# A 4096 x 4096 x 4096 matrix product with leaky ReLU: first rows of A transposed in fp32 in place of bf16 and laid out in plain rows, and one late store issued whole

## The chip, the cores and the metric

The kernel runs on one core of a Trainium2 chip. The metric is the device time of one execution in microseconds (us), lower is better. A run's profile gives in addition the span of one execution, about 1.8 us shorter than the time of that execution. Engines are named as in the profile: PE does matrix products, with its weight loads shown apart as PEld, DVE, ACT and POOL work on vectors, SP issues transfers. PE writes its results into the memory PSUM; SBUF is the memory from which it reads. The pitch of equal instructions is the time from the start of one to the start of the next.

## The reference

```python
def setup_inputs():
    m, k, n = 4096, 4096, 4096
    return {"a": randn(m, k) as float32, "b": randn(k, n) as float32, "alpha": float32(0.01)}

def reference(a, b, alpha):
    x = np.matmul(a, b)
    return np.where(x > 0, x, alpha * x)
```

The product may be computed in bf16. PE multiplies by a stationary operand that has to hold A transposed, so A is rounded to bf16 and turned on the chip.

## The kernel before

The output is made in regions of 512 x 1024; PE does 8192 matmuls of 128 x 128 by 128 x 512. Nearly all of A comes in by transfers that round on the way, and is turned by DVE. Only the first 512 x 1024 of A, with the first 1024 rows of B, take another way, because nothing can start without them: they come in as fp32 by four and eight transfers of 512 KB on the SP queue (the last of B in two halves), alternating until A is done. Each of the four row tiles of A is rounded on DVE, turned by eight PE transposes into PSUM, and copied to SBUF, half by ACT and half by DVE.

```python
ident = small_pool.tile([P, P], BF16, name="ident")
...
a_rounded = at_pool.tile([P, MT, kw0], BF16, name="a_rounded", tag="at")
order = [("a", 0), ("b", 0), ("a", 1), ("b", 1), ("a", 2), ("b", 2), ("a", 3)]
...
turned = {(i, half): psum_pool.tile([P, kc0 // 2, P], BF16, name="turned", tag="ps") ...}

def round_a(i):
    nc.vector.tensor_copy(a_rounded[:, i, :], a_in[:, i, :])

def turn_a(i):
    cols = a_rounded[:, i, :].rearrange("m (p c) -> m c p", c=kc0)
    for c in range(kc0):
        nc.tensor.transpose(turned[i, 2 * c // kc0][:, c % (kc0 // 2), :], cols[:, c, :], ident)
    for half, copy in ((0, nc.scalar.copy), (1, nc.vector.tensor_copy)):
        to = a0[:, half * kc0 // 4:(half + 1) * kc0 // 4, i * P:(i + 1) * P, :]
        copy(to.rearrange("p c m e -> p c e m"),
             turned[i, half].rearrange("p (c e) m -> p c e m", e=2))
...
# the end of each region, for each of its four row tiles
for nt in range(NP):
    cols = slice(nt * NT, (nt + 1) * NT)
    nc.scalar.activation(o[:, cols], banks[mt, nt], LRELU, alpha=alpha)
    if final:
        nc.sync.dma_start(to[:, cols], o[:, cols])
if not final:
    nc.scalar.dma_start(to, o)
```

The tile `a0` keeps two chunks of the contraction interleaved, element by element (its last axis, `e`, is 2). So the copy writes every second 2-byte element. `final` marks the last region of all, whose stores go out in halves on SP.

## Time and profile before

| what | before |
|---|---|
| time, median of 3 runs | 1785.22 us (1784.99 to 1785.26) |
| span of the profiled run | 1783.7 us |
| PE busy | 99% of the span |

The prediction shows the lines of the page and of the timeline. Read them with one question: what has to be over before PE can run without a gap, and what comes after its last matmul? The change can act only there. The chain of work that ended last (start, duration, what), in the stretch that the change touches:

```profile
1.65 6.05 DMA a_in<-in_a_dram
...
7.73 0.70 DVE a_rounded L261
...
8.48 0.72 PE turned L266 x8
...
9.22 0.73 DVE at L269
9.95 0.30 DVE bt L276
...
10.26 0.70 DVE a_rounded L261
...
14.04 0.42 PE turned L266 x4
...
14.48 0.74 ACT at L269
...
15.27 8.61 PE ps L148 x39
```

The chain starts at the landing of the second tile of A, and it goes through DVE three times: cast, copy, cast. The other is the list of waits on the SP queue near the end (who waited for whom: total us, times, longest):

```profile
SPq L424 <- DMA out_dram<-o: 1.6, 1, 1.6
```

After its last store SP waits 1.6 us for stores to land.

### The profile page before, as it was taken

The page shows a single profiled execution, that of the slowest core. Times are in us where ns is not written, and L with a number is a line of the kernel's source. Part 1 is how long each engine was busy: PE and PEld are TensorE (multiplying, and loading weights), DVE is VectorE, ACT ScalarE, POOL GpSimd, SP SyncE. Part 2 cuts the span into 40 slices and gives each one's busy share as a digit, 9 for nine tenths or more (in the row PEclk, how much of TensorE's full clock was granted, in tenths as well). Part 3 has the DMA queues.
Part 4 walks back from the last instruction along what each step waited for, and adds up shares of the span by engine and source line. Part 5 has one row for each costly group of instructions (what it writes and reads, how often), then busy time and mean ns, then how long its engine had stood idle before and what let it go on. Part 6 is the DMA issues. An engine that isn't in the chain of part 4 may idle for free.

```text
span 1783.7 us, 17979 instructions
## 1 busy us (share of the span) xinstructions
PE 1766.8 (99%) x8070; PEld 804.6 (45%) x8234; DVE 156.3 (9%) x121; ACT 152.2 (9%) x270; POOL 360.3 (20%) x663
## 2 busy tenths in 40 slices
PE   9999999999999999999999999999999999999999
PEld 4444444444444444444444444444444444444444
DVE  5530000032000000002200000000220000000000
ACT  2010000000000000000000000000000000000001
POOL 4630210433002020143201202014320110301000
PEclk9999999999999999999999999999999999999999
DMA  9994653988039164397704917449860581835511
GB/s 260 191 253 111 116 133 86 190 127 126 39 94 189 48 120 117 94 198 127 124 24 96 187 48 143 93 105 201 131 119 12 114 170 48 168 68 123 113 48 47
DMA packets 147164, 214.06 MB, mean 120 GB/s; under 512 B 12816, under 2 KB 76304, under 8 KB 147088
## 3 DMA queue, kind: packets, MB, share of 16 engines
q0 software_dynamic: 126208, 139.50, 48.3%
q10 hardware_dynamic: 17856, 65.02, 9.3%
q1 hardware_dynamic: 3024, 8.39, 1.2%
q8 instruction: 64, 1.05, 0.2%
q14 instruction: 12, 0.10, 0.0%
HBM read 285.21 MB, written 67.11 MB: 198 GB/s over the span
## 4 chain that ended last, share of the span: by engine, by line
PE 99%; issue 1%; DMA 0%; DVE 0%; ACT 0%; SPq 0%
PE ps L148 99%; DMA a_in<-in_a_dram 0%; PE turned L266 0%; ACT at L269 0%; DVE a_rounded L261 0%; DVE at L269 0%; ACT o L388 0%; SPq L248 0%; SPq L246 0%; DVE bt L276 0%
## 5 line engine op out<-in xcount | busy, mean ns | idle before, releaser
L148 PE MATMUL ps<-bt,at 128*128 128x512 bf16 x8028 | 1760.4, 379 | 10.1 <-ACT bt L276 0.6
L148 PEld LDWEIGHTS <-at 128*128 128x128 bf16 x8192 | 801.2, 98 | 968.2 <-ACT at L269 2.6
L138 POOL DMA_DIRECT2D bt<-in_b_dram x408 | 217.1, 538 | 1084.4 <-PE ps L148 895.6
L388 ACT ACTIVATE o<-ps 128x512 f32<-128x512 f32 x240 | 130.7, 595 | 1524.4 <-PE ps L148 1450.4
L121 DVE STREAM_TRANSPOSE at<-a 128x1024 uint32<-128x1024 uint32 (+1 forms) x63 | 123.0, 1989 | 1136.2 <-PE ps L148 1113.8
L116 POOL DMA_DIRECT2D a<-in_a_dram x248 | 142.4, 581 | 203.1 <-DVE at L121 139.0
L225 DVE TENSOR_TENSOR part<-ps,part 128x512 f32<-128x512 f32 x32 | 20.3, 682 | 32.0 <-PE ps L148 32.0
L228 ACT ACTIVATE o<-part 128x1024 f32<-128x1024 f32 x8 | 8.5, 1058 | 77.2 <-DVE part L225 64.6
L223 ACT COPY part<-ps 128x512 f32<-128x512 f32 x8 | 4.4, 593 | 15.1 <-PE ps L148 12.4
L221 DVE COPY part<-ps 128x512 f32<-128x512 f32 x8 | 5.1, 671 | 4.8 <-PE ps L148 4.8
L276 ACT CAST bt<-b_in 128x512 bf16<-128x512 f32 x8 | 4.8, 617 | 2.0 <-DMA b_in<-in_b_dram 2.0
L84 PE MATMUL ps<-w 128*128 128x512 bf16 x8 | 3.6, 631 | 1.2 <-DVE x L80 1.2
L266 PE MATMUL turned<-ident,a_rounded 128*128 128x128 bf16 x32 | 2.8, 230 | 1.6 <-DVE a_rounded L261 1.5
L266 PEld LDWEIGHTS <-a_rounded 128*128 128x128 bf16 x32 | 2.4, 148 | 3.6 <-DVE a_rounded L261 3.4
L276 DVE CAST bt<-b_in 128x512 bf16<-128x512 f32 x8 | 3.4, 430 | 3.7 <-DMA b_in<-in_b_dram 3.7
L269 ACT COPY at<-turned 128x512 bf16<-128x512 bf16 x4 | 2.9, 729 | 8.6 <-PE turned L266 8.6
L269 DVE COPY at<-turned 128x512 bf16<-128x512 bf16 x4 | 2.9, 734 | 3.6 <-PE turned L266 3.6
L261 DVE CAST a_rounded<-a_in 128x1024 bf16<-128x1024 f32 x4 | 2.8, 698 | 4.1 <-DMA a_in<-in_a_dram 4.0
L315 POOL CAST x<-bt 128x1 f32<-128x1 bf16 x1 | 0.2, 183 | 11.5 <-ACT bt L276 11.5
L84 PEld LDWEIGHTS <-w 128*128 128x128 bf16 x8 | 1.0, 142 | 2.8 <-issue 1.6
L81 ACT ACT_TABLE_LOAD x1 | 1.3, 1283 | 0.7 <-PEq L410 0.7
L301 PE MATMUL ps<-w 128*128 128x512 bf16 x2 | 0.6, 379 | 0.0
(10 smaller groups left out, 1.6 us busy)
## 6 DMA issues: line engine op xcount, KB each, us to landing
bt<-in_b_dram POOLq DMA_DIRECT2D x408, 256.0 KB, 7.8
out_dram<-o ACTq DMA_DIRECT2D x124, 512.0 KB, 2.9
a<-in_a_dram POOLq DMA_DIRECT2D x248, 128.0 KB, 5.2
b_in<-in_b_dram SPq DMA_DIRECT2D x7, 512.0 KB, 9.8
a_in<-in_a_dram SPq DMA_DIRECT2D x4, 512.0 KB, 6.8
out_dram<-o SPq DMA_DIRECT2D x8, 256.0 KB, 2.0
b_in<-in_b_dram SPq DMA_DIRECT2D x2, 256.0 KB, 10.5
```

The lines of the kernel that those rows point to most:

```text
L84: nc.tensor.matmul(wp, w[:, :P], w, start=True, stop=True)
L116: nc.gpsimd.dma_start(to, src.rearrange("(g i) w -> i g w", i=32))
L121: nc.vector.transpose(dst.rearrange("p c m e -> p c (m e)").bitcast(U32) .rearrange("p c (g i) -> p g c i", i=32), held[0][:, 4 * t0:4 * t ...
L138: nc.gpsimd.dma_start(new_b(pi, u)[:, c0 + c, :], b_rows(n, s, c))
L148: nc.tensor.matmul(ps, at[mb, h, u][:, c // 2, mt * P:(mt + 1) * P, c % 2], bt[pi, u][:, c, nt * NT:(nt + 1) * NT], start=first, stop=last,)
L221: nc.vector.tensor_copy(kept, banks[mt, nt])
L225: nc.vector.tensor_add(kept, banks[mt, nt], kept)
L228: nc.scalar.activation(o, part[h][:, mt, :], LRELU, alpha=alpha)
L266: nc.tensor.transpose(turned[i, 2 * c // kc0][:, c % (kc0 // 2), :], cols[:, c, :], ident)
L269: copy(to.rearrange("p c m e -> p c e m"), turned[i, half].rearrange("p (c e) m -> p c e m", e=2),)
L276: copy(b0[:, i, columns(nt)], b_in[i][:, columns(nt)])
L388: nc.scalar.activation(o[:, cols], banks[mt, nt], LRELU, alpha=alpha)
```

## The change

The intent: spare the cast of A on DVE by turning the fp32 values as they lie, and round them where they have to be copied anyway, out of PSUM. The turned tile gets its chunks side by side, so the copies write plain rows. Apart from that, the first row tile of the last region is stored whole on the ACT queue.

```diff
-    ident = small_pool.tile([P, P], BF16, name="ident")
+    ident = small_pool.tile([P, P], FP32, name="ident")
@@ matmul: the first tile is read as plain rows
+            plain(t)[:, c, rows] if (mb, h, u) == (0, 0, 0) else t[:, c // 2, rows, c % 2],
@@ PSUM tiles of the transposes
-        (i, half): psum_pool.tile([P, kc0 // 2, P], BF16, name="turned", tag="ps")
+        (i, half): psum_pool.tile([P, kc0 // 2, P], FP32, name="turned", tag="ps")
@@ no cast
-    def round_a(i):
-        nc.vector.tensor_copy(a_rounded[:, i, :], a_in[:, i, :])
     def turn_a(i):
-        cols = a_rounded[:, i, :].rearrange("m (p c) -> m c p", c=kc0)
+        cols = a_in[:, i, :].rearrange("m (p c) -> m c p", c=kc0)
 ...
-            copy(to.rearrange("p c m e -> p c e m"), turned[i, half].rearrange(...))
+            copy(plain(a0)[:, c:c + kc0 // 2, i * P:(i + 1) * P], turned[i, half])
@@ stores
-                        if final:
+                        if final and mt:
                             nc.sync.dma_start(to[:, cols], o[:, cols])
-                    if not final:
+                    if not final or mt == 0:
                         nc.scalar.dma_start(to, o)
```

(Shortened: `plain` is the view of the tile with its chunks side by side.)

More of the change, by code (lines that the diff above doesn't have):

```diff
@@ L145, in pieces_b, with plain @@
         return [lambda c=c: load_b(pi, pairs[pi], s, c) for c in range(SEGS[s][2])]
+    def plain(t):
+        return t.rearrange("p c m e -> p (c m e)").rearrange("p (c m) -> p c m", c=KC)
     def mm(ps, mb, h, pi, u, mt, nt, c, first, last):
+        rows = slice(mt * P, (mt + 1) * P)
+        t = at[mb, h, u]
         nc.tensor.matmul(
             ps,
-            at[mb, h, u][:, c // 2, mt * P:(mt + 1) * P, c % 2],
+            plain(t)[:, c, rows] if (mb, h, u) == (0, 0, 0) else t[:, c // 2, rows, c % 2],
             bt[pi, u][:, c, nt * NT:(nt + 1) * NT],
@@ L236 @@
     b_in = [b_two[c // 4][:, c % 4, :] for c in range(kc0)]
-    a_rounded = at_pool.tile([P, MT, kw0], BF16, name="a_rounded", tag="at")
     order = [("a", 0), ("b", 0), ("a", 1), ("b", 1), ("a", 2), ("b", 2), ("a", 3)]
@@ L267, in turn_a @@
         for half, copy in ((0, nc.scalar.copy), (1, nc.vector.tensor_copy)):
-            to = a0[:, half * kc0 // 4:(half + 1) * kc0 // 4, i * P:(i + 1) * P, :]
-            copy(
-                to.rearrange("p c m e -> p c e m"),
-                turned[i, half].rearrange("p (c e) m -> p c e m", e=2),
-            )
+            c = half * kc0 // 2
+            copy(plain(a0)[:, c:c + kc0 // 2, i * P:(i + 1) * P], turned[i, half])
     def round_b(i):
@@ L289, in work @@
         waiting.clear()
-    round_a(0)
     for n, (what, i) in enumerate(order):
         if what == "a":
-            if n:
-                round_a(i)
             turn_a(i)
```

## The prediction

> **What bounds the kernel now.** I read the page first (busy times, then the chain of work that ended last, then the groups), and then the timeline of the first 16 us and of the last 30, because the change touches only these.
>
> ```profile
> PE 1766.8 (99%) x8070; PEld 804.6 (45%) x8234; DVE 156.3 (9%) x121; ACT 152.2 (9%) x270; POOL 360.3 (20%) x663
> ...
> PE ps L148 99%; DMA a_in<-in_a_dram 0%; PE turned L266 0%; ACT at L269 0%; DVE a_rounded L261 0%; DVE at L269 0%; ACT o L388 0%; SPq L248 0%; SPq L246 0%; DVE bt L276 0%
> ...
> L148 PE MATMUL ps<-bt,at 128*128 128x512 bf16 x8028 | 1760.4, 379 | 10.1 <-ACT bt L276 0.6
> ```
>
> The matmuls of line 148 are 99% of the chain. Some records are missing (8028 of the 8192 that the sizes require), so I take the pitch from the chain of work in order of time, where a piece that shows 49 of them starts every 10.79 us. If one record in 50 is missing, that is 10.79 / 50 = 0.2158 us, and 8192 x 0.2158 = 1767.8 us. The span is 1783.7 us, so everything that is not these matmuls is 15.9 us, 0.9% of the span. The change adds and removes no matmul of line 148, so it can win at most a part of these 15.9 us.
>
> Where they are, the timeline of the start shows (start, duration, engine, line, operation, tiles, count, idle before and its releaser):
>
> ```profile
> 4.26 0.69 DVE L261 CAST a_rounded<-a_in 128x1024 bf16<-128x1024 f32 x1 [3.11 <-DMA a_in<-in_a_dram]
> 5.01 0.71 PE L266 MATMUL turned<-ident,a_rounded 128*128 128x128 bf16 x8 [0.22 <-DVE a_rounded L261]
> ...
> 7.73 0.69 DVE L261 CAST a_rounded<-a_in 128x1024 bf16<-128x1024 f32 x1 [0.93 <-DMA a_in<-in_a_dram]
> ...
> 8.48 0.70 PE L266 MATMUL turned<-ident,a_rounded 128*128 128x128 bf16 x8 [1.12 <-DVE a_rounded L261]
> 8.98 0.73 ACT L269 COPY at<-turned 128x512 bf16<-128x512 bf16 x1 [2.26 <-PE turned L266]
> ...
> 9.22 0.73 DVE L269 COPY at<-turned 128x512 bf16<-128x512 bf16 x1 [0.80 <-PE turned L266]
> ...
> 9.76 1.07 PE L148 MATMUL ps<-bt,at 128*128 128x512 bf16 x4 [0.58 <-ACT at L269]
> ...
> 10.26 0.69 DVE L261 CAST a_rounded<-a_in 128x1024 bf16<-128x1024 f32 x1
> ...
> 11.01 0.71 PE L266 MATMUL turned<-ident,a_rounded 128*128 128x128 bf16 x8 [0.18 <-DVE a_rounded L261]
> ...
> 12.80 0.71 DVE L261 CAST a_rounded<-a_in 128x1024 bf16<-128x1024 f32 x1
> ...
> 14.04 0.65 PE L266 MATMUL turned<-ident,a_rounded 128*128 128x128 bf16 x8
> ```
>
> Four 512 KB tiles of A land one after the other; each is rounded on DVE, turned by eight transposes, and taken out of PSUM by ACT and DVE. From 11.01 us on PE has work without a gap worth naming: what is on PE after that moment moves the end one for one. What is on it before can hide in idle time.
>
> The end, from the timeline of the last microseconds:
>
> ```profile
> 1779.72 0.60 ACT L388 ACTIVATE o<-ps 128x512 f32<-128x512 f32 x1 [1.08 <-PE ps L148]
> ...
> out_dram<-o SPq DMA_DIRECT2D x8, 256.0 KB, 2.0
> ```
>
> The last activation ends at 1780.32; the rest up to 1783.7 (3.4 us) is the last half store, which lands about 2.0 us after its issue, and the end of the program.
>
> **What the Trainium skill says.** Four places. TensorE: Matmul & The Clock Gate, Terms: the weight load and matmul instructions of trn2 have a transpose mode, "4× faster for FP32". FP8 and Floating Point Precision, TensorE Precision Notes: true FP32 takes four passes through the array; so I read the two together as one pass for a transpose in fp32. TensorE, Weight-path perf modes: the fast weight load is for 128 weights of a dtype that is not FP32, so the fp32 transposes lose it. TensorE, LDWEIGHTS: a load takes about P / 1.2 ns, 107 ns for 128 columns. The trace of before has no fp32 on PE, so it can neither confirm nor deny the first two. It does show the bf16 transposes pitched far below 107 ns: eight in 0.71 us with 0.225 for one gives (0.71 - 0.225) / 7 = 0.069 us, which agrees with a fast load there.
>
> **The change, part by part.** The order of instructions on PE stays; what changes there is that each bf16 transpose with its separate weight load becomes one fp32 instruction without a separate one, which now waits for the DMA itself.
>
> 1. Removed: four casts on DVE, 0.69 to 0.71 us each, 2.8 us. The first two lie on a path that starts with a DMA landing (7.70 us for the second tile). The later two begin the moment DVE ends other work, so their tiles may have landed a little earlier. With the cast away, the second group can start at about 7.75 in place of 8.48; then the matmuls behind it wait for the copies and for B.
> 2. Changed: the eight copies out of PSUM. Before, 0.73 us each, bf16 with a strided write. After, fp32 in and plain rows of bf16 out. The same engines take 128x512 fp32 out of PSUM in 593 ns (ACT, line 223) and 671 ns (DVE, line 221), so I take 0.60 and 0.67: 0.13 us less on ACT, 0.06 on DVE, and half of the copies lies on the path.
> 3. Added: the dearer transposes. Call x the pitch of one. Streaming 128 columns takes 128/512 of 0.2158 = 0.054 us. One pass with load and stream in turn is an estimate of 0.107 + 0.054 = 0.16 us, from the skill's load and the trace's stream. The third and fourth groups stand in dense work: 16 x (0.16 - 0.069) = 1.46 us there. The first two groups add as much, mostly into idle time.
> 4. The weights of the first tile now lie side by side. Their loads (98 ns in the mean) hide under 216 ns of matmul: nothing.
> 5. The store: one of 512 KB on the ACT queue in place of two of 256 KB on SP, seven microseconds and more before the last activation. Stores of this kind land in 2.9 us, and the buffer is wanted again only two row tiles (about 7 us) later. ACT is idle over a microsecond between activations. Nothing.
>
> Put in order with x = 0.16, spacing the landings of A and B evenly between the ones that the trace shows by a wait (7.70 and 16.64 us, seven transfers apart, so 1.28 each, and the third A tile at about 10.2): second group 7.75 to 9.03; ACT's copy ends 9.15; B's cast on ACT ends 9.77; the four matmuls end at 10.25; third group 10.3 to 11.6; ten matmuls of 0.216, with the second copy done at 11.7 and B's third cast at 12.35, end at 13.75; fourth group 13.75 to 15.03. Before, the fourth group was issued from 14.04 to 14.04 + 8 x 0.069 = 14.6. Dense matmuls follow in both, as many in each. So **0.4 us slower**: some 0.3 won up to the start of the fourth group, and 0.7 lost in it.
>
> **Rivals.** By the same working with another x:
> - Rival A, fp32 as cheap as bf16 (x = 0.07): third group at 10.2 when its tile lands, fourth at about 13.06 in place of 14.04: **1.0 us faster**, 1784.2. For it: transposes move data and do no arithmetic. Against: four bytes an element, and no fast load.
> - Rival B, the four passes apply, or loads cannot run ahead. x = 4 x 0.054 + 0.107 = 0.32: the second group ends at 10.3, the third at 13.8, the fourth at 18.5, **3.9 us slower**, 1789.1. If the load too is paid in every pass (x = 0.64), the groups fill PE from the start and the end is some 14 us later, 1799. For it: the built program keeps these transposes whole, without a separate weight load that could be pulled forward, and each waits as one.
> - Rival C, no matter what x is, the start is bound by landings: 0 within 0.3. Against: the trace shows no wait of PE for B or A after 14 us, and the last B half lands at 20.76 and is cast by about 21.2, while PE wants it at about 23, after most of the first 64 matmuls. There is no later wait to absorb a delay.
> - Rival D, the whole store makes the next activations wait for buffer or queue. The margins of point 5 speak against; were it to bite, it would be under a microsecond.
>
> **Range and chances.** x = 0.07 gives -1.0, 0.16 gives +0.4, 0.32 gives +3.9. I hold the middle likeliest and the dear side likelier than the cheap one, so I put the middle at +0.7 over the 1785.2 measured: **1785.9 us**, range **1784.0 to 1790.0**. For 2% faster, 36 us, the whole overhead of 15.9 us is too small. For 2% slower each of 32 transposes would have to cost more than a microsecond. So within 2% has 0.98, the other two 0.01 each.
>
> **What would show it right or wrong.** The group of the fp32 transposes, eight in a row: their length over eight is x, and decides between the middle and rivals A and B. No cast of A on DVE, the second group at about 7.75; the copies at 0.60 and 0.67; the end of the fourth group near 15.0. The stretch after it and the last 3.4 us unchanged. I am wrong if x lies above 0.35 or if PE shows a wait after 15 us that it did not have, or if the clock drops while PE does transposes in place of matmuls.

## The result

The changed kernel took 1785.16 us in the median (1784.53 to 1785.40, 4 runs), the kernel before 1785.24 us in the same rounds (1784.99 to 1786.42, 4 runs). Ratios in this text are the mean time of one kernel's runs over that of the other's of the same rounds, so not quite the ratio of the medians: 0.9998, 95% interval 0.998 to 1.0015. The result is correct.

The timed runs cannot tell half a microsecond apart; the traces can, because they show where a stretch begins and ends. The profile after: the row of fp32 transposes and their loads, and the copies (line, engine, operation, tiles, count, busy us and mean ns of one, idle time before).

```profile
L268 PEld LDWEIGHTS turned<-ident,a_in 128*128 128x128 f32 x32 | 4.3, 196 | 2.4 <-issue 1.2
L268 PE MATMUL turned<-ident,a_in 128*128 128x128 f32 x32 | 4.8, 296 | 0.4 <-DMA a_in<-in_a_dram 0.4
...
L271 DVE CAST at<-turned 128x512 bf16<-128x512 f32 x4 | 2.8, 692 | 10.5 <-PE turned L268 10.5
L271 ACT CAST at<-turned 128x512 bf16<-128x512 f32 x4 | 2.3, 585 | 8.7 <-PE turned L268 8.7
```

And the timeline, with the second, third and fourth group of transposes and the matmuls behind the fourth:

```profile
7.84 1.16 PE L268 MATMUL turned<-ident,a_in 128*128 128x128 f32 x8 [0.36 <-DMA a_in<-in_a_dram]
...
10.46 0.97 PEld L268 LDWEIGHTS turned<-ident,a_in 128*128 128x128 f32 x8 [0.57 <-issue]
10.49 1.13 PE L268 MATMUL turned<-ident,a_in 128*128 128x128 f32 x8
...
13.40 1.07 PEld L268 LDWEIGHTS turned<-ident,a_in 128*128 128x128 f32 x8
13.62 1.05 PE L268 MATMUL turned<-ident,a_in 128*128 128x128 f32 x8
...
14.51 9.74 PE L154 MATMUL ps<-bt,at 128*128 128x512 bf16 x42
```

The fourth group starts at 13.62 in place of 14.04, so 0.42 us earlier. The matmuls behind it start at 14.51 in place of 14.53 (the prediction's working has 14.6 for it): the group now takes 0.89 us of PE where it took 0.49. What the missing cast won on the way, the dearer transposes took back at the end of it, to 0.02 us. PE shows its own loads here, which the built program did not list apart; in the fourth group they run ahead, 0.22 us before the first transpose.

At the other end, the wait of SP for the last stores:

```profile
SPq L420 <- DMA out_dram<-o: 1.2, 1, 1.2
```

It is 0.4 us shorter. To add the two ends up, I use three marks: G, the start of the second group of transposes; C, the start of the first copy of the first 64 matmuls out of PSUM, by when PE is dense and the start is over; E, the end of the last activation. C is in these two lines, of before and after:

```profile
23.91 2.05 ACT L223 COPY part<-ps 128x512 f32<-128x512 f32 x4 [3.84 <-PE ps L148]
...
23.85 2.05 ACT L229 COPY part<-ps 128x512 f32<-128x512 f32 x4 [3.78 <-PE ps L154]
```

| trace | second A tile landed | G | C | C - landing | E | span - E |
|---|---|---|---|---|---|---|
| before | 7.70 | 8.48 | 23.91 | 16.21 | 1780.32 | 3.38 |
| after | 7.79 | 7.84 | 23.85 | 16.06 | 1780.25 | 2.94 |

(The page gives the span to 0.1 us only; span - E is taken from the times in the traces.)

From C to E both take 1756.4 us. So the span fell by 0.5 us: 0.15 less from landing to C, 0.09 more because that tile happened to land later, 0.44 less in the tail (from E to the end), 0.50 in all.

### The profile page after: what moved, and what is told of

Same layout as the page of the kernel before. It is cut to its first block, busy times and chain, and to the rows that moved or that the text cites. A ratio compares the mean times of both kernels' runs of the same rounds, so it can differ in the third digit from the quotient of the medians.

```text
span 1783.2 us, 17975 instructions
## 1 busy us (share of the span) xinstructions
PE 1768.7 (99%) x8070; PEld 806.6 (45%) x8234; DVE 153.4 (9%) x117; ACT 152.0 (9%) x270; POOL 360.1 (20%) x663
## 3 DMA queue, kind: packets, MB, share of 16 engines
q8 instruction: 64, 1.05, 0.2%
## 4 chain that ended last, share of the span: by engine, by line
PE 99%; issue 1%; DMA 0%; ACT 0%; SPq 0%; DVE 0%
PE ps L154 99%; DMA a_in<-in_a_dram 0%; PE turned L268 0%; DVE at L271 0%; ACT o L384 0%; ACT at L271 0%; SPq L253 0%; SPq L251 0%
## 5 line engine op out<-in xcount | busy, mean ns | idle before, releaser
L268 PEld LDWEIGHTS turned<-ident,a_in 128*128 128x128 f32 x32 | 4.3, 196 | 2.4 <-issue 1.2
L268 PE MATMUL turned<-ident,a_in 128*128 128x128 f32 x32 | 4.8, 296 | 0.4 <-DMA a_in<-in_a_dram 0.4
```

## The experiments

My theory after this result: the start is a near tie, because the cast's 0.75 us off the path is paid back in transposes with a pitch of about 0.11 us that lie in dense PE work. Rivals: the start is bound by landings whatever PE does; or it was the layout of the copies, not the dtype, that moved anything. For the tail: the store made it, or chance did. All experiments ran in the fast state, or as a single look whose state is called unknown. All are correct but the one that is wrong on purpose.

### Each half of the change alone

```diff
# store_only: the kernel before, with
-                        if final:
+                        if final and mt:
-                    if not final:
+                    if not final or mt == 0:
# turn_only: the changed kernel with these lines as before
# after_again: the changed kernel
```

> The kernel before with only the whole first store of the last region. My theory: the store is off the path, so the time is that of before within 0.3 us, the first copy of the first 64 matmuls out of PSUM starts at 23.9 us as before, and the tail (span less the end of the last activation) is the 3.4 us of before give or take what two looks at one kernel differ by. Rival: the store is what shortened the tail from 3.4 us in the profile of before to 2.95 us in that of after; then the tail is near 2.95 here too and the time 0.4 us lower.

> The changed kernel with the store of before (two halves on SP). My theory: the fp32 transposes alone move the time by under 0.2 us; the fourth group is issued from 13.6 to about 14.5 us, the first copy out of the first 64 matmuls starts at 23.85. Rival as for the store alone: the tail is 3.4 us here and the time 0.4 us above the whole change.

> The changed kernel once more, on the same chip and rounds as its two halves. Theory: ratio to before between 0.9995 and 1.0005, fourth group at 13.6 us, tail anywhere from 2.9 to 3.5 us if the tail is chance, 2.95 if the store made it.

| kernel | median of 5, us | ratio to before, 95% interval | G | C | C - G | span - E |
|---|---|---|---|---|---|---|
| store_only | 1785.66 | 0.9994 (0.9982 to 1.0007) | 9.07 | 24.50 | 15.43 | 2.94 |
| turn_only | 1785.80 | 0.9995 (0.9982 to 1.0007) | 8.37 | 24.38 | 16.01 | 3.38 |
| after_again | 1785.26 | 0.9992 (0.9979 to 1.0006) | 7.99 | 23.98 | 15.99 | 2.94 |

Before ran 1786.47 us in these rounds. The intervals all hold 1, so the times decide nothing; the traces do. **The tail follows the store**: 2.94 with the whole store, 3.38 without, so my theory that it does nothing fell. (Over all traces of this text the tail is 3.38 or 3.39 in the five with halves and 2.94 or 2.95 in the eight with the whole store; the exception, 3.19, was made on purpose, below.) In these traces the stretch C - G is the same to 0.02 us for one kind of transpose: 15.43 with bf16 (before too), 15.99 to 16.01 in fp32 (after too). G follows the landing by 0.77 us with the cast (0.78 before) and by 0.04 to 0.05 without. Together that is the 0.15 us: 0.73 won by the missing cast, 0.58 lost after it. The second tile landed anywhere between 7.7 and 8.3 us, which shifts a whole run by more than the change does; my expectation of a fixed C was too simple.

### What the store changes: the last of eight waits

The build shows what the store could have to do with it. A semaphore is a counter that an instruction can wait for. Such transfers count on eight semaphores, 0 to 7, in turn. At its end SP waits for all eight, one after the other. With two half stores in place of one whole, the last store of the program falls on number 0; with one transfer fewer it falls on number 7. Then all waits before it are over when it lands, where otherwise seven more follow it. The traces have these waits. Before, all eight pass after the landing; after, seven of them are over by 1781.1 us (kind, count, duration in ns, first and last start):

```profile
L424 SPq EVENT_SEMAPHORE  x8: 27/28/28, 1782.4 to 1782.8; - x8
...
L420 SPq EVENT_SEMAPHORE  x7: 28/28/28, 1780.7 to 1781.1; - x7
L420 SPq EVENT_SEMAPHORE  x1: 28/28/28, 1782.3 to 1782.3; - x1
```

From the first to the eighth it takes 1782.80 - 1782.37 = 0.43 us before, 0.061 for each of seven. The wait for the last store itself passes 2.06 us after E before and 2.04 us after E in the changed kernel, so that store lands equally late, to 0.02 us. A test that keeps the store whole, yet moves the last store to another semaphore, tells this from the store itself:

```diff
# lane_three: the changed kernel; four transfers more, in the middle of the program
+                    if r == 5:
+                        for nt in range(NP):
+                            cols = slice(nt * NT, (nt + 1) * NT)
+                            nc.scalar.dma_start(to[:, cols], o[:, cols])
-                    if not final or mt == 0:
+                    elif not final or mt == 0:
                         nc.scalar.dma_start(to, o)
```

> The changed kernel, first store of the last region whole as there, but the four stores of one region in the middle of the program issued in halves: four transfers more, so that the last store of the program counts on the fourth of the eight semaphores that such transfers use in turn (numbered 0 to 7), in place of the eighth; before it was the first. At the end SP waits for the eight one after the other. Theory: the tail (span less the end of the last activation: 3.4 us in all looks with the store in halves, 2.9 to 3.0 in all with it whole) is set by how many of these waits still follow the one for the last store: 7 of them made 0.45 us, 0.064 each, so 4 of them give 2.93 + 0.26 = 3.19 us, though the store is whole. Rival: it is the whole store itself (fewer transfers near the end, a free SP queue): then 2.93 us stays.

The wait of SP in its trace:

```profile
SPq L424 <- DMA out_dram<-o: 1.4, 1, 1.4
```

Its span is 1784.3 us and its last activation ends at 1781.11, so the tail is **3.19 us, as expected** (to the last digit partly by rounding: a wait costs 0.061 us, not 0.064). The wait for the last store passes 2.05 us after E here too, and four more follow it. The whole store by itself does nothing; its number in the row of transfers does. The time was 1785.58 us, ratio to before 0.9997 (0.9984 to 1.0009). In the profiled run a later piece of A landed at 24.70 us and held PE up for about 0.5 us between C and E; that is outside the tail.

### What a transpose costs, and where

```diff
# first_twice, fourth_twice (i == 0, i == 3), on the changed kernel;
# fourth_twice_bf16 the same for i == 3 on the kernel before
         for c in range(kc0):
-            nc.tensor.transpose(turned[...], cols[:, c, :], ident)
+            for _ in range(2 if i == 3 else 1):
+                nc.tensor.transpose(turned[...], cols[:, c, :], ident)
```

> The changed kernel with each transpose of the first group done twice (the second overwrites the same values). Theory: the first group stands in time that PE spends waiting for the second tile of A (landed at 7.8 us), so its 1.0 us more is hidden up to 0.2 us: the second group starts by 8.1 us, the first copy out of the first 64 matmuls by 24.1. Rival: every transpose counts one for one: 24.85.

> The changed kernel with each transpose of the fourth group done twice. Theory: that group stands in dense work, so 8 x 0.122 = 0.98 us more on PE moves the first copy out of the first 64 matmuls from 23.85 to about 24.8, and the span by as much. Rival (the start is bound by the landing of B): under 0.3 us.

> The kernel before with each bf16 transpose of the fourth group done twice. Theory: 8 x 0.069 = 0.55 us, so the first copy out of the first 64 matmuls starts at about 24.45 in place of 23.91. The difference to the same experiment in fp32, 0.43 us, is the dearer pitch of a group on the path. Rival: the pitch of the second transpose of the same chunk is no better in bf16 than in fp32, and it costs about 1 us too.

Doubling the first group changed nothing that can be seen: G at 7.95, C at 23.77, span 1783.1.

```profile
4.58 2.04 PE L269 MATMUL turned<-ident,a_in 128*128 128x128 f32 x16
...
7.95 1.05 PE L269 MATMUL turned<-ident,a_in 128*128 128x128 f32 x8
```

Doubling the fourth group, in fp32 and then in bf16:

```profile
13.71 1.93 PE L269 MATMUL turned<-ident,a_in 128*128 128x128 f32 x16
15.48 1.75 PE L154 MATMUL ps<-bt,at 128*128 128x512 bf16 x6
...
15.91 1.16 PE L267 MATMUL turned<-ident,a_rounded 128*128 128x128 bf16 x16
```

From the start of the fourth group to C it took 24.82 - 13.71 = 11.11 us, where the changed kernel took 23.85 - 13.62 = 10.23: 0.88 us for eight transposes, **0.110 us each**. In bf16 the same was 26.29 - 15.91 = 10.38 against 23.91 - 14.04 = 9.87: 0.51 us, **0.064 each**. The starts of the single transposes in the traces agree: 0.111 us apart in the fourth group of the changed kernel, 0.061 before. So transposes in the fourth group count one for one, those of the first are free, and the start there is not bound by landings: that rival is out. The difference, 0.37 us for the eight, is the price of fp32 in this group.

The absolute C of the bf16 run (24.45 expected) was missed by far, for a reason of its own: see the control below.

### Whether the transpose mode and the spacing matter

```diff
# plain_matmul: an ordinary fp32 product with the identity
-            nc.tensor.transpose(turned[...], cols[:, c, :], ident)
+            nc.tensor.matmul(turned[...], cols[:, c, :], ident, start=True, stop=True)
# near_columns: 128 columns side by side; wrong result on purpose
-        cols = a_in[:, i, :].rearrange("m (p c) -> m c p", c=kc0)
+        cols = a_in[:, i, :].rearrange("m (c p) -> m c p", c=kc0)
```

> The changed kernel with the transposes as ordinary fp32 matmuls by the identity, without the transpose mode. Theory: the mode is what makes one pass do; without it each takes four passes, a pitch of 0.43 us or more[...], the second to fourth groups 2.5 us longer each or more, the first copy out of the first 64 matmuls at 30 us or later and the span 6 to 12 us longer. Rival: the mode makes no difference, the pitch stays 0.12 us and the time is unchanged. The result stays right.

> The changed kernel with the transposes reading 128 columns of A that lie side by side, in place of every eighth (32 bytes apart). The result is wrong on purpose: chunks of A and B no longer match. Theory: the pitch of 0.122 us is that of a load of 128 fp32 columns, whatever their spacing; it stays within 0.01. Rival: the spacing costs; the pitch falls to 0.07 to 0.11 and the fourth group ends 0.1 to 0.4 us earlier.

The fourth group without the transpose mode:

```profile
20.91 3.87 PE L268 MATMUL turned<-ident,a_in 128*128 128x128 f32 x16
```

Eight transposes now leave sixteen records, and a group takes 3.87 us. With 0.40 for one record, the pitch of a record is (3.87 - 0.40) / 15 = 0.231 us, of a transpose 0.46 us, 4.2 times the 0.110. C came at 33.97 and the span became 1793.3 us, 10.1 more than with the mode, within the 6 to 12 expected. So the mode is worth a factor of four here, and without it the change would have cost about 10 us.

With columns side by side (a relative error of 0.23) the load's record shrank from 193 to 140 ns in the median, but the fourth group took 1.04 us in place of 1.05. The spacing does not set the pitch.

### The layout alone

```diff
# layout_only: the kernel before, bf16 and casts as they were, but
-            to = a0[:, half * kc0 // 4:(half + 1) * kc0 // 4, i * P:(i + 1) * P, :]
-            copy(to.rearrange("p c m e -> p c e m"), turned[i, half].rearrange(...))
+            c = half * kc0 // 2
+            copy(plain(a0)[:, c:c + kc0 // 2, i * P:(i + 1) * P], turned[i, half])
```

> The kernel before with only the layout of the first transposed tile changed: bf16 transposes and casts on DVE as before, but chunks side by side, so that the copies out of PSUM write plain rows. Theory: the strided write of 2-byte elements made the copies 0.73 us; they come to about 0.6 on both engines, the fourth group stays near 14.0 us and the first copy out of the first 64 matmuls starts 0.1 us earlier. Rival: it was the bf16 in PSUM that made them slow, and they stay at 0.73.

Its copies out of PSUM:

```profile
L275 ACT COPY at<-turned 128x512 bf16<-128x512 bf16 x4 | 2.3, 586 | 9.3 <-PE turned L272 9.3
L275 DVE COPY at<-turned 128x512 bf16<-128x512 bf16 x4 | 1.7, 425 | 3.5 <-PE turned L272 3.5
```

The strided write had made them 0.73 us, so the rival, bf16 in PSUM, is out. ACT comes to the same 0.586 as in the changed kernel, and DVE to 0.425, well below the 0.692 that it needs for fp32. (The Trainium skill, VectorE: DVE Perf Modes, Why PSUM operands drop a tier, caps a copy out of PSUM at twice the plain rate, and at the plain rate in fp32; 0.425 against 0.692 us agrees.) The second tile landed at about 8.20 and C was at 24.10: 15.90 us, so **0.3 us less than before and 0.16 less than the whole change** over the same stretch. And there it was the third tile that held it up: its chain starts with that tile's landing at 10.72. So the 0.3 us is, if anything, too low. One look only, and its time of 1785.69 us says nothing by itself. But it points to the layout as the part of the change at the start that pays, and to fp32 (the missing cast, the dearer transposes and the slower DVE copies together) as a part that takes some of it back.

### Holding matmuls back, and a control

```diff
# hold_two: the changed kernel; after the third chunk of B two pairs wait, not one
-            kept = waiting.pop() if len(waiting) > 1 else None
+            back = 2 if i == 2 else 1
+            kept = waiting[-back:] if len(waiting) > 1 else []
```

> The changed kernel with two (tile, chunk) pairs, four matmuls in place of two, held back until after the fourth group. Theory: the fourth group starts 2 x 0.216 = 0.43 us earlier, at about 13.2, if its tile has landed by then, and the four matmuls behind it cover most of the 0.95 us from its start to its copies, so that the first copy out of the first 64 matmuls starts about 0.35 us earlier, at 23.5, and the time falls by 0.35 us. Rival: the fourth tile lands only about 13.6, which the changed kernel's order hides; then nothing is won and PE shows a wait for the DMA before the fourth group.

The fourth group came 13.62 - 10.92 = 2.70 us after the third, against 13.62 - 10.49 = 3.13: 0.43 less, as expected. From the third group to C it was 13.07 us against 13.36, so 0.29 won of the 0.35. But the third tile landed late, PE waited for it, and C came at 23.99. The time was 1785.11 us, ratio to before 0.9991 (0.9978 to 1.0003), against 1785.26 of the changed kernel in the same rounds: not told apart. My rival was right in kind, with the third tile in place of the fourth.

The kernel before, as a control, because its runs had scattered more than those of its variants:

> The kernel before, unchanged, as a control: in the last timed rounds before ran 1785.9 to 1788.1 us and its variants, with the same transposes, 1785.1 to 1786.2. If that is the order in which kernels run in a round, this copy runs faster than before in the same rounds, by some 0.3 us (the gap of 0.8 between the store alone and before, less the 0.45 us that its tail explains); if it is the kernel, the copy scatters as before does. In the trace the tail is 3.4 us and the second group of transposes starts 0.75 us after its tile lands.

The copy took 1786.26 us (1785.67 to 1786.93), before 1785.97 (1785.46 to 1786.78): ratio 1.0 (0.9987 to 1.0014), so no effect of order is seen. But its trace showed what the one before had not. The table by stretches (us, its length, then busy time of PE, PEld, DVE, ACT and POOL, the granted PE clock, the DMA share, GB/s):

```profile
10.00:11.00 1.00, 1.00 (x3) 0.36 (x4) 0.97 (x3) 0.34 (x1) 0.00 (x0) 0.50 0.99 393
11.00:12.00 1.00, 1.00 (x6) 0.54 (x5) 0.14 (x1) 0.00 (x0) 0.00 (x0) 0.50 1.03 406
12.00:13.00 1.00, 1.00 (x9) 0.61 (x6) 0.29 (x1) 0.72 (x2) 0.00 (x0) 0.58 1.01 414
```

For 3.41 us, from 9.44 to 12.85 in the trace's record of the clock, PE ran at half clock: the four matmuls before the third group took 1.89 us in place of 1.07, and C - G was 24.70 - 8.64 = 16.06 in place of 15.43. The bf16 run with the doubled fourth group had the same, from 11.46 to 14.88 us, and that is why its C was late. The Trainium skill (TensorE: Matmul & The Clock Gate, Part 1) describes a gate that halves the clock after an idle window of about 3.4 us, of windows that run freely. The 0.50 and the 3.41 us agree, but PE was not idle in the 3.41 us before: it was busy for 1.88 us of them in the copy and for 1.64 us in the other run.

This is no rarity, and I had overlooked it. The record lists the mean clock of nearly every run. One such stretch takes 3.41 x 0.5 / 1784 = 0.001 off the mean, and the traces confirm the reading: these two runs are listed at 0.999, the twelve other traces, which don't have the stretch, at 1.000. **Of 32 runs with bf16 transposes, 17 are listed at 0.999 or 0.998; of 28 with fp32 ones (plain_matmul among them), none.** In rounds that both kinds shared it is 8 of 14 against 0 of 15, and 7 of 14 against 0 of 5. It is also why before scattered: with its copy, it took 1785.76 us in the median of 11 runs at 1.000, 1786.48 of 11 at 0.999, 1787.97 of 3 at 0.998. The mean of these 25 runs is 0.6 us above the mean of the 11 at 1.000. So these stretches went with the change; what that is worth in the mean lies within the intervals of the ratios.

Why it does is argued, not shown. Between 6 and 8 us PE is busy 0.75 us before and 1.33 us after, so the dearer transposes, or their earlier start, may keep the clock up. But the busy share alone doesn't decide: the trace of store_only has two stretches of 3.41 us (4.67 to 8.08 and 8.08 to 11.50) with PE busy for 1.84 and 1.76 us, and its clock stayed up.

## Why the prediction was right or wrong

**The range and the bound were right; the direction was not.** Nothing here can win more than the 15.9 us beside the matmuls, and the measured 1785.16 us lies in the range. That range was 6 us wide, so this proves little of the steps. The middle was a loss, 0.4 us by the working and 0.7 as put (1785.9 us, 0.7 too high); the traces show a gain of 0.5. Two terms did it, both to the dear side: the pitch of the transposes and the tail. By its steps:

- **Point 1, the casts.** Held. The second group started 0.05 us after the landing, at 7.84 against 7.75 foretold.
- **Point 2, the copies.** The sizes held: 0.585 and 0.692 us against 0.60 and 0.67. But the layout experiment shows that it is the plain rows that speed ACT up, and that DVE would need only 0.425 us for bf16. The prediction did not ask what of the gain was layout alone.
- **Point 3, the transposes.** The kind was right, dearer than bf16 and far from four passes, but the size was off. x was put at 0.16 us, a load and a stream in turn; it is 0.110. (By the prediction's own ruler, the length of a group over eight, it would read 1.05 / 8 = 0.13, because the length of the last record is in it.) The skill's figure for a load of 128 columns, 107 ns (TensorE, LDWEIGHTS), alone would have been near, as if the stream of 0.054 us hid behind the next load. That it does is not shown: a load and a stream of some 0.054 us each, in turn, would give the same. What the trace shows is that the pitch follows PE's clock: the program's first matmuls are 0.427 us apart, twice the 0.216, and the first fp32 transposes, which come right after them, 0.213. The term for two groups was put at 1.46 us; with 0.110 and the bf16 pitch of 0.064 it is 16 x 0.046 = 0.74. In place of "0.3 won, 0.7 lost" it was 0.42 won up to the fourth group and 0.40 lost in it; that group ended at 14.67, foretold near 15.0.
- **Point 4, the weights side by side.** Held: the loads of the matmuls are 98 ns in the mean, before and after.
- **Point 5, the store.** Wrong. The margins for buffer and queue were right, and rival D did not bite, but "nothing" overlooked what the build does at the end: 0.44 us, from seven waits of 0.061 us each.
- **The clock.** The prediction named a drop while PE does transposes as a sign of being wrong. None came with fp32, in 28 runs. That it comes before, in about half of the runs, the one trace of before didn't show.
- **The rivals.** By the 0.6 us of the traces below, A (1.0 faster) came nearer than the middle, but by luck: not through a pitch of 0.07, but through the tail. B fell: the loads do run ahead, and a transpose in the mode takes a quarter of the time without it (0.110 against 0.46 us), as the skill's two places together said. C fell for groups on the path and holds for the first one. It was also wrong that PE has no gap from 11 us on: in both kernels it waits about 0.3 us after the fourth group, for the copies.

The sum with measured terms: -0.15 at the start, -0.44 in the tail, so 0.6 us faster for the same landing at full clock. The medians give 0.1 us in the first rounds and 1.2 in the second (1785.26 of after_again against 1786.47). Before's three runs at 1.000 in the second, 1785.86 to 1786.33 us, have a median of 1786.02 and leave about 0.8. With a tile whose landing alone moves a run by up to 0.8 us, this fits and is no proof.

Open: the layout alone together with the last store on the eighth semaphore should win 0.3 and 0.44 us over before in a run at full clock. I did not run it; 0.04% is below what the timed runs resolve, and with bf16 transposes it may meet the half clock, which costs as much. Also open is why the second tile lands anywhere from 7.7 to 8.5 us.

## What to carry to other kernels

A cost in an idle stretch is free, and the same cost in a dense stretch counts in full: doubling an instruction in each place tells which one you are in. When a change has two effects, such as dtype and layout, try each alone, since one may pay for the other. And half a microsecond of a long kernel is read from the distance between two marks in traces, not from medians of times. Where runs list their mean clock, sort the times by it first: what looks like scatter may be two states.

## What the Trainium skill lacked or had wrong

- The end of a program (no page of those I read has it): SP waits in turn for the eight semaphores of the transfers, and each wait behind the one for the last store costs 0.061 us; the tail was 3.38 to 3.39 us with the last store on the first, 3.19 on the fourth, 2.94 to 2.95 on the eighth.
- TensorE: Matmul & The Clock Gate, Part 4 (PE-mode transpose): it gives times for one transpose, not a pitch, and none for fp32. Here eight in a row are 0.110 us apart in fp32 and 0.064 in bf16. The Terms' "4× faster for FP32" agrees: 0.46 us without the mode.
- The same page, LDWEIGHTS: the 107 ns are near the pitch of 0.110 us, but the trace's record of one fp32 load reads 140 ns for columns side by side and 193 ns for every eighth, at the same pitch.
- The same page, Part 1: it does not say how busy PE may be in a window that counts as idle. Here the clock fell after 3.41 us with PE busy for 1.88 and 1.64 us, and stayed up after 1.84 and 1.76.
- ScalarE: Activation LUTs: it does not speak of the spacing of what is written. A copy of 128x512 bf16 took ACT 0.729 us into every second element and 0.586 into plain rows.
